# One attention band per query block instead of two: 128 wrapped weights, the 129th key in pass 3

## The chip, the cores and the metric

The kernel runs on one core of a Trainium2 chip. The metric is the device time of one launch in microseconds (us). TensorE (PE) multiplies matrices into PSUM banks, VectorE (DVE), ScalarE (ACT) and GpSimd (POOL) do the elementwise work, and SyncE (SP) issues every DMA of this kernel in one queue.

## The reference

One layer of a decoder for 2048 tokens of width 1024, in float32. After an RMS norm, one projection gives q, k, v and gate_B (8 heads of 64 each) and u, v, gate of a gMLP branch. The attention has three branches; each is a causal band over dilated keys:

```
DILATIONS = ((128, 1), (512, 4), (2048, 16))     # (window, dilation)
# query t attends t - dilation*j, j = 0..window/dilation  (129 keys: 128 back, and itself)
scores = q.k / 8;  keys outside the band or before the start are masked
out, lse = softmax per branch;  the three outs are summed with weights softmax(lse)
mixed = concat(attention * silu(gate_B), gmlp * silu(gate));  h = x + mixed @ w_out
h = h + sigmoid(RMSNorm(h) @ W_g + b_g) * (p @ W_p)
```

For a block of 128 queries the band covers parts of two key blocks: of its own block the keys up to the query, of the block behind it the keys from the query's position on. The 129th key (j = 128) lies at the query's own position in the block behind: 128 tokens back in branch 0, 512 in branch 1. In branch 2 the sequence has no block behind.

## The kernel before

Matrices are float32 numbers split into a high and a low part, so a projection of one 128-row tile to 512 columns is 24 matmuls of 128x512 (`project`, L230; `gm_product`, L633, in the gMLP).

- **Pass 1** takes 16 row tiles. `prep` norms and transposes a tile; `step` (four per tile, q k v g) projects it and hands the PSUM bank to `post_qk`, `post_v` or `post_gb`. The banks: q "mm" (2), k "s" (2), v and g take turns in "av" and "gt" (1 each). `turn_qk` transposes q and k by DMA (L434), copies k once more on ACT (L437) and stores both to DRAM.
- **The passage** into pass 2 loads and splits three gMLP weight groups (`load_group`, L136 and L138), and starts the gMLP products. The attention's buffers take the place of pass 1's.
- **Pass 2** has a hand-written order on PE (`manual_schedule`); the other engines follow the scheduler. There are 152 steps (4 head pairs x 3 branches). A step is one query block with both key blocks (108 of them), or one or two blocks with only their own key block; it has two heads and up to 512 weights per query row. `Step.scores`: 4 or 8 float16 matmuls (L762), a masked minimum from PSUM on DVE (L765), a constant added on DVE (L771), exp on ACT (L773). One step later `Step.turn`: a float16 copy on ACT (L780), the rest on POOL (L117), a DMA transpose to `pt` (L783). Six steps after the scores `Step.values`: 65-column matmuls (L794). After each `turn`, `fill(1.3)` puts gMLP matmuls of about 1.3 us into PE's order; `fill(18)` stands ahead of the first step. 13 of the 16 gMLP tiles run here, 3 after it (`tail`).
- **Pass 3** merges the three branches of a tile (`merge`: small DVE operations, L567, three POOL operations L569 to L572), transposes the result by DMA through the tiles `tm` (`turn_mixed`, L182 to L197) into the single buffer `aT`, and does `out_proj` and `gate`. The merge runs up to two tiles ahead.

Of the kernel before, what the change touches and what calls it, by code (L numbers as in the profile page):

```python
# [13 lines left out]
I32 = mybir.dt.int32  # L14
U16 = mybir.dt.uint16
# [21 lines left out]
def _shape_constants():  # L37

    p = np.arange(128)

    def mask(keys, back=False):
        keep = keys[None, :] >= p[:, None] if back else keys[None, :] <= p[:, None]
        return np.where(keep, 0, NEG).astype(np.float32)
    k0 = p.reshape(32, 4).T.reshape(128)
    return {"c_ident": np.eye(128, dtype=np.float32),
            "c_mask": np.concatenate([mask(k0, True), mask(k0), mask(p, True), mask(p)], 1),
            "c_freq": INV_FREQ.reshape(1, 32)}
# [3 lines left out]
PR, PH, OB, SV = 3, 6, 5, 5  # L51

LAG_B, LAG_C = 1, 6

BLOCK0, FILL = 18, 1.3
# [26 lines left out]
def hybrid_layer(ctx: ExitStack, tc: tile.TileContext, io, out):  # L82
# [17 lines left out]
    d_gb = dram.tile([S, 512], F32, name="d_gb")  # L100
    d_at = dram.tile([NT, 128, D], F32, name="d_at")
# [5 lines left out]
    cst.tile([128, 8], F32, name="pad")  # L107
    bs = cst.tile([128, 4], F32, name="bs")
# [13 lines left out]
    def load_group(src, c0, slot, stage, on_dve, each=None, gain=None):  # L122
# [3 lines left out]
        while k < nk:  # L126
# [5 lines left out]
            for i in range(n):  # L132
                hi, lo = slot[:, 0, k, :], slot[:, 1, k, :]
                if gain is not None:
                    nc.vector.tensor_scalar(raw[:, i], raw[:, i], gain[:, k:k + 1], None, op0=OP.mult)
                nc.scalar.activation(hi, raw[:, i], AF.Copy)  # L136
                dve = (k * on_dve) // 8 != ((k + 1) * on_dve) // 8
                (nc.vector if dve else nc.gpsimd).tensor_tensor(lo, raw[:, i], hi.bitcast(F32),  # L138
                                                                op=OP.subtract)
# [116 lines left out]

    AT, GT, XT, slots = {}, {}, {0: xt0}, {}
    usc = cst.tile([128, 1], F32, name="usc")

# [14 lines left out]
    with ExitStack() as s1, ExitStack() as s1q:  # L274
# [90 lines left out]
        def v_scale():  # L365
# [3 lines left out]
            ones = p1.tile([128, 128], F32, name="ones")  # L369
# [37 lines left out]
        def post_qk(n, which, ps):  # L407
# [8 lines left out]
            m1 = p1.tile([128, HEADS, 2, 32], F32, name="m1", bufs=2)  # L416
# [6 lines left out]
            pool_tt(f1, f1, f2, OP.add)  # L423
            r = m1.rearrange("p h t d -> p h (t d)")
            nc.vector.tensor_tensor(r, r, rs[:, :, None].to_broadcast([128, HEADS, 64]), op=OP.mult)
            hl = p1.tile([128, HEADS, 2, 64], F16, name="hl", bufs=2)
            nc.scalar.activation(hl[:, :, 0], r, AF.Copy)
            nc.vector.tensor_tensor(hl[:, :, 1], r, hl[:, :, 0], op=OP.subtract)
            return hl

        def turn_qk(n, which, hl):
# [3 lines left out]
            if which:  # L435
                sp = hl.rearrange("p h t d -> p h (t d)")
                nc.scalar.activation(sp.rearrange("p h (r i) -> p h r i", r=4),  # L437
                                     st.rearrange("p h (i r) -> p h r i", r=4), AF.Copy)
                st = sp
            nc.sync.dma_start(d_qk[which][:, n // 4, :, n % 4 * 128:n % 4 * 128 + 128], st)  # L440

        def post_v(n, ps):
# [4 lines left out]
            nc.scalar.activation(vt[:, :, 0, 0:64], z, AF.Copy, scale=sv)  # L447
            nc.vector.scalar_tensor_tensor(vt[:, :, 1, 0:64], z, sv, vt[:, :, 0, 0:64],
                                           op0=OP.mult, op1=OP.subtract)
            nc.sync.dma_start(d_vt[:, n * 128:(n + 1) * 128].rearrange("q p e -> p q e"),  # L450
# [3 lines left out]
        def post_gb(n, ps):  # L454
            g = p1g.tile([128, 512], F32, name="gb")
            nc.scalar.activation(g, ps, AF.Tanh, scale=0.5)
# [5 lines left out]
        def gm_constants():  # L462
            for name, src in (("mask", io["c_mask"]), ("wsT", d_ws),
                              ("lng", bcast(io["ln_v_g"], 512)), ("lnb", bcast(io["ln_v_b"], 512))):
                CG[name] = pg.tile([128, 512], F32, name=name)
                nc.sync.dma_start(CG[name], src)

        def spatial_weights():
# [4 lines left out]
            nc.sync.dma_start(keep[:, 0:128], io["c_mask"][:, 384:512])  # L473
# [486 lines left out]
```

## Time and profile before

| what | value |
|---|---|
| median of 3 runs | 1287.59 us (1286.81 to 1293.2) |
| profiled execution | 1287.08 us, span 1285.3 us, granted clock 0.985 |
| busy over the span | PE 93%, DVE 69%, ACT 50%, POOL 40% |
| DMA queue | 440432 packets, 232.44 MB |

Read it by stage. Pass 1 lasts to about 390 us, the passage to 430, pass 2 to 811, a second passage (the gMLP's last tiles, the weights of pass 3) to 950, pass 3 to the end. A share over the whole span mixes these.

### The profile page before, as it was taken

The numbers are of one execution on the slowest core, as the hardware profiler recorded it, in microseconds if no ns is written. First come the engines' busy times: TensorE is split into PE (matmuls) and PEld (weight loads), VectorE is DVE, ScalarE is ACT, GpSimd is POOL, SyncE is SP. The second block draws the span as 40 slices with busy tenths as digits, with TensorE's granted clock in tenths as the row PEclk, the third lists the DMA queues.
The fourth block names the chain that finished last, engine by engine and source line by source line (L and its number), as shares of the span: only waits on it lengthen the run. The fifth ranks groups of instructions, "written<-read, shape, count | busy, mean of one in ns | idle before, by whom it ended". The sixth has DMA issues, their size and how long they took to land.

```text
span 1285.3 us, 21313 instructions
## 1 busy us (share of the span) xinstructions
PE 1200.1 (93%) x7166; PEld 972.2 (76%) x7166; DVE 892.9 (69%) x2253; ACT 648.0 (50%) x1273; POOL 511.6 (40%) x454
## 2 busy tenths in 40 slices
PE   6899999999996899999899899869999999999998
PEld 4678787777785687777678688758778888888887
DVE  6895565565466588888778678598766776766733
ACT  5654433433335477777677677444334434434422
POOL 4762333343354365665555556342212212121200
PEclk9999999999999899999999999999999999999999
DMA  7498787768669989999999999845454565654531
GB/s 266 142 221 210 166 180 173 163 167 177 152 165 255 238 190 228 222 237 223 224 229 232 230 215 225 213 164 176 142 147 121 152 174 128 156 162 132 140 90 50
DMA packets 440542, 233.80 MB, mean 182 GB/s; under 512 B 337136, under 2 KB 389104, under 8 KB 440432
## 3 DMA queue, kind: packets, MB, share of 16 engines
q1 hardware_dynamic: 440432, 232.44, 75.5%
q8 instruction: 56, 0.92, 0.3%
q14 instruction: 54, 0.44, 0.1%
HBM read 102.99 MB, written 57.54 MB: 125 GB/s over the span
## 4 chain that ended last, share of the span: by engine, by line
PE 38%; DMA 21%; DVE 16%; ACT 8%; issue 7%; POOL 5%; SPq 4%; DVEq 0%; ACTq 0%; POOLq 0%
PE mm L230 17%; DMA pt<-raw 7%; PE mm L633 7%; PE gt L230 6%; DMA xt<-raw 3%; DMA st<-hl 3%; PE s L230 3%; PE s L762 2%; PE pt L794 2%; DVE wslot L138 2%; ACT pr L773 2%; ACT raw L182 2%; DVE raw L186 1%; DVE aT L197 1%; DMA raw<-w_in 1%
## 5 line engine op out<-in xcount | busy, mean ns | idle before, releaser
L230 PE MATMUL mm<-wslot,aT 128*128 128x512 f32 x1536 | 361.4, 390 | 5.1 <-ACT aT L196 1.9
L230 PEld LDWEIGHTS mm<-wslot,aT 128*128 128x128 f32 x1536 | 287.8, 188 | 67.8 <-ACT aT L196 3.4
L633 PE MATMUL mm<-wslot,aT 128*128 128x512 f32 x1152 | 312.7, 412 | 24.0 <-DVE gv L624 19.3
L633 PEld LDWEIGHTS mm<-wslot,aT 128*128 128x128 f32 x1152 | 210.3, 194 | 63.7 <-DVE gv L624 20.1
L117 POOL TENSOR_TENSOR raw<-pr,raw 128x512 f16<-128x512 f32 (+1 forms) x152 | 178.0, 1176 | 142.8 <-ACT raw L780 125.0
L230 PE MATMUL gt<-wslot,aT 128*128 128x512 f32 x744 | 183.9, 402 | 9.1 <-DVE gb L457 8.8
L773 ACT ACTIVATE pr<-pr,ost 128x256 f32<-128x256 f32 (+1 forms) x384 | 150.2, 451 | 72.2 <-DVE ost L771 66.6
L230 PEld LDWEIGHTS gt<-wslot,aT 128*128 128x128 f32 x744 | 143.5, 194 | 43.0 <-DVE gb L457 10.9
L794 PEld LDWEIGHTS <-pt 128*128 128x128 f16 x1800 | 64.9, 98 | 64.6 <-DMA pt<-raw 35.3
L780 ACT ACTIVATE raw<-pr 128x512 f16<-128x512 f32 (+1 forms) x152 | 93.1, 620 | 33.6 <-DMA pt<-raw 31.0
L794 PE MATMUL pt<-sv,pt 128*128 128x65 f16 x1800 | 82.0, 194 | 22.5 <-DMA pt<-raw 20.2
L765 DVE CUSTOM_DVE_ANT_0 pr<-s,mask 128x256 f32<-128x256 f32 (+1 forms) x256 | 81.1, 357 | 20.7 <-POOL raw L117 16.2
L230 PE MATMUL av<-wslot,aT 128*128 128x512 f32 x360 | 87.2, 394 | 7.5 <-DVE gb L457 4.1
L230 PE MATMUL s<-wslot,aT 128*128 128x512 f32 x384 | 91.0, 391 | 0.0
L117 POOL TENSOR_TENSOR m<-m,m 128x512 f32<-128x512 f32 x32 | 47.7, 1491 | 101.3 <-DVE rsh L150 95.0
L230 PEld LDWEIGHTS av<-wslot,aT 128*128 128x128 f32 x360 | 67.2, 188 | 24.9 <-DVE gb L457 6.0
L230 PEld LDWEIGHTS s<-wslot,aT 128*128 128x128 f32 x384 | 72.5, 189 | 15.3 <-ACT wslot L136 0.3
L572 POOL TENSOR_TENSOR ma<-ob,ma 128x512 f32<-128x512 f32 x16 | 23.8, 1488 | 123.4 <-DMA ma<-d_gb 87.3
L762 PEld LDWEIGHTS <-sq 128*128 128x128 f16 x768 | 70.1, 120 | 3.5 <-issue 1.6
L569 POOL TENSOR_TENSOR ob<-ob 128x512 f32<-128x512 f32 x16 | 21.0, 1314 | 128.8 <-DVE ob L567 128.8
L762 PE MATMUL s<-sk,sq 128*128 128x256 f16 (+1 forms) x512 | 72.3, 277 | 0.0
L771 DVE TENSOR_SCALAR ost<-ost 128x2 f32<-128x2 f32 (+1 forms) x152 | 65.4, 432 | 2.6
(198 smaller groups left out, 1730.0 us busy)
## 6 DMA issues: line engine op xcount, KB each, us to landing
xt<-x SPq DMA_DIRECT2D x32, 512.0 KB, 4.5
d_o<-ost SPq DMA_DIRECT2D x48, 264.0 KB, 3.7
raw<-w_in SPq DMA_DIRECT2D x38, 256.0 KB, 3.4
sv<-d_vt SPq DMA_DIRECT2D x32, 264.0 KB, 3.6
ob<-d_o SPq DMA_DIRECT2D x16, 528.0 KB, 4.6
xt<-d_at SPq DMA_DIRECT2D x16, 512.0 KB, 4.5
sk<-d_k SPq DMA_DIRECT2D x32, 256.0 KB, 4.8
out<-th SPq DMA_DIRECT2D x32, 256.0 KB, 2.8
```

The costliest lines, as they stand in the source:

```text
L117: nc.gpsimd.tensor_tensor(dst, a, b, op=op)
L138: (nc.vector if dve else nc.gpsimd).tensor_tensor(lo, raw[:, i], hi.bitcast(F32), op=OP.subtract)
L182: nc.scalar.activation(turned[t].bitcast(U16), words[:, t], AF.Copy)
L230: nc.tensor.matmul(ps, aT[:, ha, k, :], w(slot, hw, k), start=(n == 0), stop=(n == 3 * nk - 1))
L572: nc.gpsimd.tensor_tensor(m, o, m, op=OP.mult)
L633: nc.tensor.matmul(ps, GT[c][:, ha, k, :], slots[g][:, hw, k, :], start=(n == 0), stop=(n == 23))
L762: nc.tensor.matmul(ps[:, c:c + nk], cols(br, j, Q[h]), cols(br, j, K, n, h, self.nb), start=(n == 0), stop=(n == 1))
L765: nc.vector.tensor_tensor_reduce(pr[:, c:c + nk], ps[:, c:c + nk], mask[:, m - nk:m], -1.0, 3e38, op0=OP.add, op1=OP.min, accum_out=o[:, j ...
L771: nc.vector.tensor_scalar(nm, nm, math.log(PSCALE), None, op0=OP.add)
L773: nc.scalar.activation(pr[:, c:c + nk], pr[:, c:c + nk], AF.Exp, bias=o[:, j - j0, 130 + h:131 + h], scale=-1.0)
L780: nc.scalar.activation(ph, pr[:, :width], AF.Copy)
L794: nc.tensor.matmul(PO[0][:, j % 2, h], self.pt[:, t, c // 128], vt[:, h, vv, 0:65], start=(n == 0), stop=(n == 3 * self.nb - 1))
```

## The change

- **Wrapped band.** The scores of both key blocks are still computed. Where the own block's key lies after the query, DVE copies the score of the same column of the block behind over it in PSUM (`copy_predicated`), so 128 scores per query and head are left. DVE takes their maximum, ACT adds the constant, and ACT's exp reads PSUM.
- **Pairs.** Two row tiles share one `turn`: one float16 copy, one POOL subtraction, one DMA transpose for 512 weights. There are 192 steps and 96 turns.
- **Parting.** Five steps after the turn (`part`, for the 56 pairs with a block behind) DVE cuts the own block's weights out of `pt` into `pc` (a bitwise and over 32-bit words) and POOL subtracts them from `pt`. `values` multiplies `pc` with the own block's v and `pt` with the block behind's; the number of matmuls stays.
- **Far key.** Pass 1 multiplies q of a tile with k of the tiles 1 and 4 back (POOL), sums per head (DVE) and stores the 27 results; it also stores v in float32. Pass 3's merge takes the two scores as two more branches with denominator 1 and loads the rows of v: 1 or 2 more loads, 2 or 4 more POOL operations a tile, and some five more small DVE operations.
- **Pass 1.** g takes "pt" (2 banks) from the third tile on, so v has "av" and "gt" alone. The store of q and k (with ACT's copy of k) is issued behind the first ACT operation of the next step's `post`.
- **Passage.** The splits of the three gMLP weight groups come behind named operations of the last tiles' `post`. `fill` ahead of the first step is 11, after a step 0.93 (own block alone) or 1.17.

```diff
-LAG_B, LAG_C = 1, 6
-BLOCK0, FILL = 18, 1.3
+LAG_B, LAG_P, LAG_C = 1, 6, 9
+BLOCK0, FILL = 11, (0.93, 1.17)
...
+                with ExitStack() as behind:
+                    for ins in after:
+                        behind.enter_context(tc.issue_after(ins))
+                    nc.scalar.activation(hi, raw[:, i], AF.Copy)
...
+        def late(after):
+            for f in LATE:
+                with tc.issue_after(after):
+                    f()
+            LATE.clear()
...
+        def far_scores(n):
+            far = small.tile([128, 2, HEADS], F32, name="far", bufs=1)
...
+                    pool_tt(f, RT["k", n - back], RT["q"][1], OP.mult)
+                    nc.vector.tensor_reduce(far[:, x], t, axis=AX.X, op=OP.add, negate=True)
+            nc.sync.dma_start(d_far[n], far)
...
-            ps = bank({"q": "mm", "k": "s", "v": ("av", "gt")[n % 2], "g": "pt" if n >= NT - 2 else ("gt", "av")[n % 2]}[g])
+            ps = bank({"q": "mm", "k": "s", "v": ("av", "gt")[n % 2], "g": "pt" if n > 1 else ("gt", "av")[n]}[g])
...
+            nc.gpsimd.tensor_tensor(t, t, w[:, 3 + x][:, :, :, None].to_broadcast([128, 4, 2, 64]), op=OP.mult)
+            nc.gpsimd.tensor_tensor(o, o, t, op=OP.add)
...
+            def part(self, br, after):
...
+                with tc.issue_after(after.ins):
+                    nc.vector.tensor_tensor(d, a, bits[:, None, None, m:m + 64].to_broadcast([128, 2, 2 * n, 64]),
+                                            op=OP.bitwise_and)
+                pool_tt(a, a, d, OP.subtract)
...
+                    own = ps[:, :, 128:256]
+                    nc.vector.copy_predicated(own, m.bitcast(U32)[:, None].to_broadcast([128, 2, 128]),
+                                              ps[:, :, 0:128])
+                    self.last = nc.vector.tensor_reduce(top, own, axis=AX.X, op=OP.max, negate=True)
...
-                nc.vector.tensor_scalar(nm, nm, math.log(PSCALE), None, op0=OP.add)
+                nc.scalar.activation(top, top, AF.Copy, bias=math.log(PSCALE))
+                for h in range(2):
+                    nc.scalar.activation(pr[:, h], own[:, h], AF.Exp, bias=top[:, h:h + 1],
+                                         scale=1.0 if nb == 2 else -1.0)
...
+                if 0 <= n - LAG_P < len(plan) and steps[n - LAG_P].i:
+                    steps[n - LAG_P].pair.part(steps[n - LAG_P].br, steps[min(n, len(plan) - 1)].last)
```

## Rows read from the trace of the kernel before

**Rows 1.** Stages: stretch; us, busy us (instructions) per engine, clock, DMA share, GB/s.

```profile
90.00:390.00 300.00, 287.11 (x1241) 234.17 (x1240) 176.72 (x317) 120.74 (x201) 119.34 (x118) 0.99 0.75 176
390.00:430.00 40.00, 27.15 (x113) 22.01 (x113) 23.32 (x36) 18.83 (x31) 14.47 (x12) 0.83 0.89 241
430.00:811.00 381.00, 358.85 (x3484) 287.47 (x3483) 304.48 (x1191) 273.01 (x614) 228.91 (x199) 0.99 1.07 224
950.00:1250.00 300.00, 300.00 (x1325) 248.42 (x1324) 200.99 (x373) 120.16 (x219) 54.48 (x46) 1.00 0.54 144
```

**Rows 2.** Waits of PE, 90 to 390 us: total us, times, longest.

```profile
PE gt L230 <- DVE gb L457: 8.8, 5, 2.7
PE av L230 <- DVE gb L457: 4.1, 4, 1.4
```

**Rows 3.** Timeline of one pass 1 tile: start, us, instruction, idle before.

```profile
198.88 5.73 PE L230 MATMUL gt<-wslot,aT 128*128 128x512 f32 x24 [1.27 <-DVE gb L457]
...
222.25 2.11 PE L230 MATMUL av<-wslot,aT 128*128 128x512 f32 x8 [1.31 <-DVE gb L457]
```

**Rows 4.** Waits of ACT, 90 to 390 us.

```profile
ACT hl L437 <- DMA st<-hl: 38.3, 11, 4.9
```

**Rows 5.** Timeline of the passage.

```profile
395.96 11.04 PE L633 MATMUL mm<-wslot,aT 128*128 128x512 f32 x48
...
415.14 0.59 ACT L456 ACTIVATE gb<-pt 128x512 f32<-128x512 f32 x1
...
419.85 8.21 PE L633 MATMUL mm<-wslot,aT 128*128 128x512 f32 x24 [12.85 <-DVE gv L624]
...
423.06 0.80 SPq L264 DMA_DIRECT2D sq<-d_q  x2
```

**Rows 6.** Waits of PE's weight loads, 430 to 811 us.

```profile
PEld L794 <- DMA pt<-raw: 34.6, 33, 3.9
PEld L794 <- issue: 28.4, 104, 0.5
```

**Rows 7.** Timeline of PE's weight loads in one step of pass 2.

```profile
596.86 1.24 PEld L633 LDWEIGHTS mm<-wslot,aT 128*128 128x128 f32 x6
598.37 0.42 PEld L794 LDWEIGHTS <-pt 128*128 128x128 f16 x12 [0.27 <-issue]
```

**Rows 8.** Groups by form, 430 to 811 us: busy us, mean ns; idle before.

```profile
L117 POOL TENSOR_TENSOR raw<-pr,raw 128x512 f16<-128x512 f32 x146 | 173.1, 1190 | 130.1 <-ACT raw L780 112.4 <-POOL raw L117 5.6 <-issue 5.2
...
L780 ACT ACTIVATE raw<-pr 128x512 f16<-128x512 f32 x146 | 90.4, 626 | 33.5 <-DMA pt<-raw 31.0
...
L765 DVE CUSTOM_DVE_ANT_0 pr<-s,mask 128x256 f32<-128x256 f32 x144 | 55.2, 416 | 16.1 <-POOL raw L117 14.4 <-PE s L762 1.2
...
L771 DVE TENSOR_SCALAR ost<-ost 128x2 f32<-128x2 f32 x110 | 50.1, 457 | 1.8
...
L197 DVE TENSOR_TENSOR aT<-xt,aT 128x512 fp32r<-128x512 f32 x26 | 31.4, 1219 | 0.0
```

**Rows 9.** Groups by form, whole span.

```profile
L117 POOL TENSOR_TENSOR m<-m,m 128x512 f32<-128x512 f32 x32 | 47.7, 1491 | 101.3 <-DVE rsh L150 95.0 <-DVE m L420 6.2
...
L558 ACT ACTIVATE w<-w 128x24 f32<-128x24 f32 x16 | 3.6, 222 | 59.3 <-DVE w L557 59.3
```

**Rows 10.** DMA issues: count, median us to landing.

```profile
pt<-raw SPq DMA_TRANSPOSE x152, 4.1
```

**Rows 11.** Timeline of one pass 3 tile.

```profile
1021.39 0.77 ACT L196 ACTIVATE aT<-tm 128x256 fp32r<-128x256 f32 x2 [1.44 <-DVE tm L186]
...
1022.32 5.60 PE L230 MATMUL mm<-wslot,aT 128*128 128x512 f32 x24
...
1027.76 5.60 PE L230 MATMUL gt<-wslot,aT 128*128 128x512 f32 x24
...
1037.24 1.97 DVE L197 TENSOR_TENSOR aT<-tm,aT 128x256 fp32r<-128x256 f32 x2
...
1037.57 1.36 POOL L570 TENSOR_TENSOR ob<-ob 128x512 f32<-128x512 f32 x1
```

More of the change, by code (lines that the diff above doesn't have):

```diff
@@ L107, in hybrid_layer @@
     cst.tile([128, 8], F32, name="pad")
+    small.tile([128, 64], F32, name="pad", bufs=1)
     bs = cst.tile([128, 4], F32, name="bs")
@@ L589, in mixed @@
         nc.sync.dma_start(mx[0], d_gb[rows])
-        merge(ob, mx[0])
+        vr = pm.tile([128, D], F32, name="vr")
+        for x, back in enumerate(FAR):
+            if n >= back:
+                nc.sync.dma_start(vr[:, 512 * x:512 * x + 512], d_vr[(n - back) * 128:(n - back + 1) * 128])
+        merge(ob, mx[0], n, vr)
         AT[n] = mx
@@ L683, in gmlp @@
                     yield 0.43 if f is not gm_g else 1.28
[L685 to L686 removed]
+        for c, g, last in ((5, "va", (NT - 2, "k")), (4, "ua", (NT - 1, "k")), (6, "ga", (NT - 1, "v"))):
+            slots[g] = load_group(w_in, 512 * c, new_slot(), stage, WD2, after=POST[last])
         gm = gmlp()
@@ L754, in scores @@
             def scores(self):
                 Q, K = self.qk
-                br, nk, o, j0 = self.br, self.nk, self.o, self.j0
-                m = 512 if br else 256
-                ps = bank("s" if self.tick % 3 else "av")
-                self.pr = pr = p2.tile([128, 512], F32, name="pr", bufs=PR)
-                for c, j, h in self.segs:
-                    for n in range(2):
-                        nc.tensor.matmul(ps[:, c:c + nk], cols(br, j, Q[h]),
-                                         cols(br, j, K, n, h, self.nb), start=(n == 0), stop=(n == 1))
@@ new lines, in scores @@
+                m = mask[:, 128:256] if br else mask[:, 0:128]
+                ps = bank("s" if self.tick % 3 else "av")[:, 0:256 * nb].rearrange("p (h k) -> p h k", h=2)
+                pr = self.pair.pr[:, self.i]
+                for h in range(2):
+                    for n in range(2):
+                        nc.tensor.matmul(ps[:, h], cols(br, j, Q[h]),
+                                         cols(br, j, K, n, h, nb), start=(n == 0), stop=(n == 1))
+                top = o[:, j - j0, 130:132]
@@ new lines, in scores @@
+                if nb == 2:
+                    own = ps[:, :, 128:256]
+                    nc.vector.copy_predicated(own, m.bitcast(U32)[:, None].to_broadcast([128, 2, 128]),
+                                              ps[:, :, 0:128])
+                    self.last = nc.vector.tensor_reduce(top, own, axis=AX.X, op=OP.max, negate=True)
+                else:
+                    own = pr
+                    for h in range(2):
+                        self.last = nc.vector.tensor_tensor_reduce(
+                            pr[:, h], ps[:, h], m, -1.0, 3e38, op0=OP.add, op1=OP.min,
+                            accum_out=top[:, h:h + 1])
@@ L791, in values @@
+                if i == 0:
+                    PO[0] = bank("pt", (128, 2, 2, 65))
+                for h in range(2):
                     n = 0
-                    for vt in self.v[j]:
+                    for w, v in zip((self.pair.pc, self.pair.pt) if self.nb == 2 else (self.pair.pt,), self.v):
                         for t, vv in ((0, 0), (0, 1), (1, 0)):
-                            nc.tensor.matmul(PO[0][:, j % 2, h], self.pt[:, t, c // 128], vt[:, h, vv, 0:65],
+                            nc.tensor.matmul(PO[0][:, i, h], w[:, t, i, h], v[:, h, vv, 0:65],
@@ L805, in hybrid_layer @@
         quads = [(hp, br, j0) for hp in range(4) for br in (0, 2, 1) for j0 in range(0, NT, 4)]
-        plan = [(q, j) for q in quads for j in range(q[2], q[2] + 4, 2 if first(q[1], q[2] + 3) else 1)]
+        plan = [(q, j) for q in quads for j in range(q[2], q[2] + 4)]
         clock = [0.0, 0.0]
```

195 lines of the change are left out of this document (118 added, 77 removed).

## The prediction, made before the changed kernel was run

> **What bounds the kernel now.** I read the granted clock first (0.985, one core), then the stages, then in each stage what PE waits for. In pass 3 PE is busy all 300 of 300 us, and 24 matmuls follow the last 24 after 5.44 us (1022.32 to 1027.76), 227 ns each [rows 1, 11]. That is what a matmul of 128x512 costs when nothing is late, so nothing but later or fewer matmuls moves pass 3. In the other stages PE has holes: 12.9 us in pass 1, 12.9 us in the passage, where the clock is 0.83 besides, and 22.2 us in pass 2 [rows 1]. The change takes no matmul away. It can win only in those holes, 48 us and what the clock costs, and lose where it makes new ones.
>
> **Pass 1.** PE waits 12.9 us in nine places for DVE L457, g's last reader, to free the bank that v needs [rows 2]. From one v projection to the next it is 23.37 us (198.88 to 222.25), 4 x 5.44 = 21.76 are matmuls, so 1.6 us a tile is lost [rows 3]; over the eleven tiles 3 to 13 that is 18 us. Why is g's reader late? ACT stands 38.3 us in front of L437, until the DMA transpose of k has landed [rows 4], and g's tanh is queued behind it. The change treats both: g gets banks of its own, and L437 goes behind the next step's first ACT operation. Added in this pass are 27 products on POOL at about 1.49 us [rows 9], 40 us over 16 tiles beside 119 busy of 300 [rows 1]; 27 sums of 512 on DVE at no more than 1.22 us and 16 copies on ACT at 0.63 [rows 8]; two stores more per tile on SP, one of 256 KB and one of 8 KB. No engine gets near PE's 96%, so I count the work as hidden; without that cover the two products would put 3.0 us into the wait of k's rope on POOL. Bounds: 0 (something else in these in-order queues holds the 23.4 us) and -18. I take -13, nearer to the recorded idle.
>
> **The passage.** PE ends the first two gMLP products at 407 and waits 12.85 us for DVE L624, then runs 24 matmuls in 8.21 us in place of 5.6, at the lower of its two clock levels (1.2 GHz, the granted clock of the stretch is 0.83). The tanh of the last g tile, whose matmuls ended at 396, runs at 415.14, because ACT works through splits that wait for their loads; the attention's loads stand behind it on SP (423.06) [rows 5]. The change holds the splits back behind the last `post` operations and asks for 7 us less gMLP work ahead of the first step. If tanh comes 8 us sooner the loads do too, and PE, with less filler, still waits some of that. Bounds: -15 (wait and slow clock gone) and +7 (the loads come no sooner, and the 7 us of filler are missing). I take -6.
>
> **Pass 2, what goes.** PE's weight loads wait 34.6 us in 33 places for the transpose `pt` [rows 6]. Of each such wait 0.27 us would be there anyway (below), so 34.6 - 33 x 0.27 = 25.7 us are lost. The transposes compete in a DMA queue whose engines are busy 1.07 of the time, against 0.54 in pass 3 [rows 1]. 152 of them become 96 [rows 10], and with each of the 56 go an ACT copy (626 ns) and the POOL subtraction (1190 ns) that stand ahead of it [rows 8]. The lag from turn to use stays at about 14 us (7 steps of 2.0 us, before 5 of 2.4). So I count the 25.7 us as gained; if the DMA queue stayed full, none of it.
>
> **Pass 2, what comes on PE.** After a run of gMLP matmuls the next float16 weight load starts 0.27 us late, 104 times [rows 6]: six loads take 1.24 us, then 0.27 us pass, 1.51 for 6 x 0.227 = 1.36 us of matmuls [rows 7]. One more run thus costs 0.15 to 0.27 us, and 192 steps have 40 more than 152: 6 to 11 us, I take 8. The Trainium skill (TensorE: Matmul & The Clock Gate, Part 2) says that PE pulls the next weight load ahead of running matmuls; the rows show that it doesn't at this switch, and by the rule the sum would be 1254.
>
> **Pass 2, what comes beside it.** For a block with two key blocks DVE did two masked minima of 256 (416 ns each) and one constant (457) [rows 8]. Now it copies under a mask and reduces, both over 256 from PSUM. The trace has no masked copy: nearest is the minimum with a mask, 416 ns; it may cost the double if the target is read as well, and no row speaks for less. Half a `part` comes on top: 512 words with two SBUF inputs, 0.83 us at the minimum's rate and 1.22 by L197, which has two SBUF inputs as well [rows 8]. So 0.83 + 0.5 = 1.3 us against 1.29, in a step of about 2 us (381 / 192). The constant moves to ACT, 192 x 0.222 = 43 us [rows 9], against 152 x 0.45 = 68 on DVE. A two-element operation doesn't need 457 ns; it waits for something, and POOL is busy 60% of this pass [rows 1]. The Trainium skill (ScalarE: Activation LUTs, Rules for kernel authors) sends adds to VectorE; by these rows it is the dearer place here, and in neither case does it reach PE. POOL swaps 56 subtractions of 1.19 us for 56 over 32-bit words, between 1.2 and, for an unknown integer path, 3 us; I take the float row 1.49 [rows 9], +17 us on 229 of 381. The parting must be done in two steps after its scores; DVE (0.9 + 0.8 us) and POOL (1.5 us and a queue of about 1) need 4.2 of some 5.5 us (two steps and one more run of filler). That is thin. Queued behind a late `part` on DVE are the next scores' reductions, which free banks for PE. For new waits I take 8 us (56 parts at 0.15), bounds 0 and 40 (0.7 each). Sum of pass 2: -25.7 + 8 + 8 = -10, bounds -20 and +25.
>
> **Pass 3 and the passage before it.** The merge gets up to four POOL operations more (4 x 1.49 = 6 us a tile [rows 9]) and some five small DVE ones (1 us). POOL is busy 54 of 300 us [rows 1], so there is room, but not everywhere: `aT`'s first half was ready at 1022.16, out_proj started at 1022.32, 0.16 us of slack [rows 11]. DVE's L197, in front of the next transposes, took 1.97 us for two tiles of 256 while POOL ran L570 [rows 11]; more POOL work lengthens it. The merge's loads, two or three more per tile, stand on SP ahead of nothing that PE needs within a tile. Four is my estimate for both stages, bounds 0 and +36.
>
> **Sum**, against the profiled execution of 1287.1 us (the median of the runs shown is 0.5 above): 1287.1 - 13 - 6 - 10 + 4 = 1262.
>
> **Rivals.**
> - *Better throughout* (10%): all holes close. Pass 1 -18, passage -13, pass 2 -18, pass 3 0: 1238. For it: the waits named are few and the change touches each. Against: the thin margin of `part`.
> - *New waits take the place of the old in pass 2* (13%): the masked copy costs double or POOL's integer subtraction over 2.5 us, and the steps with two key blocks become bound by DVE or POOL. 108 of them at 0.14 us are +15 in place of -10: 1287, 1278 to 1292. For it: DVE 304 busy of 381 [rows 1]; against it: POOL's 112 us of waiting for ACT L780 [rows 8], room that the pairs leave.
> - *Slower, by the merge in pass 3* (12%): POOL's four operations fall just where DVE transposes the merged tile. If L197 and the copies behind it each wait for one more POOL operation, 3 us a tile, then twelve tiles lose 36 us with 0.16 to 2 us of slack: 1287 - 29 + 36 = 1294, up to 1305. It decides from 2.4 us a tile. For it: L197's 1.97 us; against: POOL's 54 us of 300 [rows 1], and three more of its operations a tile end before the next. The Trainium skill states the mechanism (GPSIMD Engine Reference, Key points): GpSimd shares its SBUF interfaces with VectorE where an instruction has two SBUF inputs. The trace agrees: 1.22 us for L197 at 512 elements in pass 2 [rows 8], 1.97 for two of 256 beside L570.
> - *Pass 1 doesn't get faster* (9%): the 23.4 us a tile are the loop through ACT, the DMA transposes and POOL, not the bank, and the products of the far key fill what `late` frees. 1262 + 13 = 1275, to 1285.
> - *No late start for the 40 new runs* (3 of the forecast's 56%): 8 us less, 1254. Against it stand 104 late starts [rows 6]; for it, that 48 of 152 runs show none of their own, most of them behind a wait for `pt`.
> - The forecast itself (56%): 1250 to 1276.
>
> **Numbers.** What a measurement here can tell from no change is about 0.5%, 6.4 us. Faster by more: the forecast 56, the better one 10, pass 1 held 5, new waits 3: 0.74. Within: 4 of pass 1, 8 of new waits, 2 of the merge: 0.14. Slower: 2 and 10: 0.12. The range of 1238 to 1293 leaves out some 5% below and 10% above; the forecast's own is 1250 to 1276.
>
> **What would show it.** Right: no wait of PE for L457, pass 1's projections of v 21.8 to 22.3 us apart; PE's first attention matmul before 415 us; 96 transposes, DMA share of pass 2 near 0.85, waits for `pt` under 10 us; some 40 more late starts of 0.27 us; PE without holes in pass 3. Wrong: waits of PE for `pt` or `pc` released by POOL's subtraction, a masked copy above 0.6 us, POOL integer work above 2 us, waits for `aT` in every tile of pass 3.

## The result, and the profile after

The changed kernel takes 1319.95 us (median of four runs, 1316.43 to 1324.45) against 1287.2 for the kernel before (four runs, 1285.2 to 1293.2): a ratio of 1.0252, 95% interval 1.0227 to 1.0277. It is slower by 2.5%; I had forecast 1262, faster by 2%. The profiled execution took 1316.43 us, its span 1314.7.

Read first by where the difference arises, with three marks that both traces have: PE's first attention matmul, the first product of the gMLP's tail, the end.

| stretch | before, us | after, us | difference |
|---|---|---|---|
| start to first attention matmul | 430.6 | 423.4 | -7.2 |
| pass 2 | 397.3 | 389.6 | -7.8 |
| tail of the gMLP, pass 3 | 457.4 | 501.8 | +44.4 |

Of the last row, 39.2 us arise in pass 3, behind a run of 48 matmuls that both have (at 934.4 and 924.6 us). The other 5.2 lie in the passage before it; no run looked into them. The stages of the changed kernel, as in [rows 1]:

```profile
90.00:390.00 300.00, 290.52 (x1271) 240.05 (x1270) 195.35 (x350) 127.22 (x212) 156.29 (x146) 0.98 0.78 191
390.00:430.00 40.00, 23.99 (x78) 16.20 (x77) 20.48 (x33) 21.51 (x40) 12.72 (x10) 0.74 1.01 276
430.00:811.00 381.00, 372.75 (x3596) 295.82 (x3595) 305.24 (x889) 259.94 (x751) 242.50 (x203) 1.00 0.86 190
950.00:1250.00 300.00, 273.50 (x1147) 221.52 (x1146) 203.40 (x375) 106.13 (x194) 118.07 (x87) 0.96 0.52 144
```

PE, busy 300 of 300 us in pass 3 before, is busy 273.5, at a clock of 0.96; POOL's busy time doubled from 54 to 118, no more than 40% of the stretch. What PE waits for there (all waits from 940 us on: total, times, longest):

```profile
PE mm L241 <- ACT aT L207: 23.2, 11, 5.2
PE mm L241 <- DVE xt L680: 3.5, 1, 3.5
```

Twelve times a projection waits for its operand or its bank. In five places the next 24 matmuls then take 7.35 to 8.59 us in place of 5.6, at a granted clock of 0.64 to 0.77 in these stretches, 10.9 us more together, so 26.7 us of waits cost 37.6. The longest of the five:

```profile
1109.14 8.59 PE L241 MATMUL mm<-wslot,aT 128*128 128x512 f32 x24 [4.36 <-ACT aT L207]
```

Pass 2 did what was asked of it. The waits of PE's weight loads, as in [rows 6], and the new forms, as in [rows 8]:

```profile
PEld L892 <- issue: 36.2, 133, 0.4
PEld L892 <- POOL pt L125: 6.1, 7, 2.2
PEld L892 <- DVE pc L837: 3.8, 3, 1.8
PEld L892 <- DVE ost L875: 2.2, 8, 0.3
PEld L892 <- DVE ost L871: 2.2, 8, 0.3
```

```profile
L125 POOL TENSOR_TENSOR pt<-pt,pc 128x512 int32<-128x512 int32 x52 | 67.9, 1307 | 50.1 <-issue 15.7 <-DVE pc L837 10.0 <-PE s L864 9.3
...
L837 DVE TENSOR_TENSOR pc<-pt,bits 128x512 int32<-128x512 int32 x52 | 48.3, 931 | 3.6 <-DMA pt<-raw 3.6
...
L879 ACT ACTIVATE ost<-ost 128x2 f32<-128x2 f32 x189 | 37.9, 200 | 90.3 <-DVE ost L871 59.2 <-DVE ost L875 29.5
...
L869 DVE COPY_PREDICATED s<-mask,s 128x256 f32<-128x256 uint32 x70 | 29.5, 421 | 4.8 <-PE s L864 4.0
```

No load waits for a transpose any more (33 did, 34.6 us); 29 more runs start late with nothing named (issue), 7.8 us in all; ten new waits, for POOL's subtraction and for `pc`, take 9.9 us. The rows that name another DVE operation, 34 loads and 9.3 us, have 0.27 us each: by their length the same late start. The masked copy costs 421 ns, the integer subtraction 1307.

Pass 1 has no wait for the bank [rows 2], and one new one, late:

```profile
PE mm L241 <- ACT aT L207: 9.5, 1, 9.5
```

### The profile page after: what moved, and what is told of

It is laid out like the page before. It is cut to its first block, busy times and chain, and to the rows that moved or that the text cites. A ratio compares the mean times of both kernels' runs of the same rounds, so it can differ in the third digit from the quotient of the medians.

```text
span 1314.7 us, 21431 instructions
## 1 busy us (share of the span) xinstructions
PE 1215.0 (92%) x7166; PEld 975.1 (74%) x7166; DVE 937.0 (71%) x2036; ACT 641.9 (49%) x1425; POOL 638.9 (49%) x535
## 5 line engine op out<-in xcount | busy, mean ns | idle before, releaser
L241 PE MATMUL mm<-wslot,aT 128*128 128x512 f32 x1536 | 378.2, 402 | 44.8 <-ACT aT L207 34.3
L705 PE MATMUL mm<-wslot,aT 128*128 128x512 f32 x1152 | 325.4, 417 | 16.6 <-ACT wslot L148 8.5
L125 POOL TENSOR_TENSOR raw<-pr,raw 128x512 f16<-128x512 f32 x96 | 115.7, 1205 | 71.9 <-ACT raw L821 44.3
L241 PE MATMUL gt<-wslot,aT 128*128 128x512 f32 x600 | 145.9, 397 | 0.2 <-ACT wslot L148 0.2
L637 POOL TENSOR_TENSOR vr<-vr,w 128x512 f32<-128x512 f32 x27 | 49.1, 1837 | 106.3 <-DVE w L626 106.3
L125 POOL TENSOR_TENSOR pt<-pt,pc 128x512 int32<-128x512 int32 (+1 forms) x56 | 70.9, 1266 | 55.4 <-issue 15.7
L879 ACT ACTIVATE ost<-ost 128x2 f32<-128x2 f32 x192 | 38.5, 200 | 93.2 <-DVE ost L871 60.5
L241 PE MATMUL pt<-wslot,aT 128*128 128x512 f32 x336 | 78.4, 389 | 0.0
L640 POOL TENSOR_TENSOR ma<-ob,ma 128x512 f32<-128x512 f32 x16 | 23.8, 1486 | 105.7 <-DMA ma<-d_gb 96.8
L241 PEld LDWEIGHTS pt<-wslot,aT 128*128 128x128 f32 x336 | 63.1, 188 | 13.1
L224 ACT ACTIVATE aT<-xt 128x1024 fp32r<-128x1024 f32 x32 | 34.0, 1061 | 66.3 <-DVE xt L680 63.9
L821 ACT ACTIVATE raw<-pr 128x512 f16<-128x512 f32 x96 | 60.4, 629 | 2.6
```

The costliest lines, as they stand in the source:

```text
L125: nc.gpsimd.tensor_tensor(dst, a, b, op=op)
L224: nc.scalar.activation(aT[:, 0].rearrange("p k t -> p (k t)"), xt, AF.Square, accum_out=ss)
L241: nc.tensor.matmul(ps, aT[:, ha, k, :], w(slot, hw, k), start=(n == 0), stop=(n == 3 * nk - 1))
L637: nc.gpsimd.tensor_tensor(t, t, w[:, 3 + x][:, :, :, None].to_broadcast([128, 4, 2, 64]), op=OP.mult)
L640: nc.gpsimd.tensor_tensor(m, o, m, op=OP.mult)
L705: nc.tensor.matmul(ps, GT[c][:, ha, k, :], slots[g][:, hw, k, :], start=(n == 0), stop=(n == 23))
```

## The experiments

Every ratio is to the kernel before, run on the same chip beside it; times are medians.

**Is it the merge, and which part of it?** The first run has the old merge (no far loads, no far weights); the second only loses these lines:

```diff
-            nc.gpsimd.tensor_tensor(t, t, w[:, 3 + x]..., op=OP.mult)
-            nc.gpsimd.tensor_tensor(o, o, t, op=OP.add)
```

> The changed kernel with the merge of the kernel before in pass 3: no loads of the far keys' scores and values there, weights for three blocks, none of the four added POOL operations. The far keys' share of the output is left out; pass 1 still computes and stores it. Pass 3 cost 390.1 us in the changed kernel against 350.9 before. Theory A (the merge is what costs) and theory B (its loads and small operations on DVE cost, not POOL's four operations) both expect pass 3 back at 350 to 356 us and 1276 to 1284 in all. Rival C (something that pass 1 or pass 2 leaves behind, such as the shorter slack of the output's loads, slows pass 3) expects 1305 or more.

> The changed kernel without POOL's two products and two sums of the far keys in pass 3; their loads, the weights for five blocks and all the small operations on DVE stay. The far keys' values are left out of the output. Theory A (POOL's four operations make DVE's copies and subtractions of the next tile late, and stand before POOL's own power for the norm) expects most of the 39 us back: 1278 to 1290. Theory B (loads on SP's queue and ten more small operations on DVE) expects 1308 to 1318.

Measured: 1277.66 us, ratio 0.990 (0.9871 to 0.993), and 1280.85, 0.9919 (0.9892 to 0.9947). Both lie in the ranges of theory A. Tail and pass 3 take 466.2 and 464.9 us against 501.8 (457.4 before). So four POOL operations a tile, 6.3 us of an engine that is idle 60% of the stretch, cost 37 us with all that waits behind them; the loads and small operations in pass 3 little or nothing. Groups of the run without them, 950 to 1250 us (busy us, mean ns), ahead of those of the changed kernel:

```profile
L208 DVE TENSOR_TENSOR aT<-tm,aT 128x256 fp32r<-128x256 f32 x48 | 29.0, 645 | 0.0
...
L629 DVE TENSOR_TENSOR ob<-ob,w 128x1536 f32<-128x1536 f32 x11 | 19.4, 1760 | 1.1
```

```profile
L637 POOL TENSOR_TENSOR vr<-vr,w 128x512 f32<-128x512 f32 x22 | 39.2, 1803 | 91.3 <-DVE w L626 91.3
L208 DVE TENSOR_TENSOR aT<-tm,aT 128x256 fp32r<-128x256 f32 x44 | 38.6, 918 | 0.0
...
L638 POOL TENSOR_TENSOR ob<-ob,vr 128x512 f32<-128x512 f32 x22 | 29.4, 1335 | 1.6
L629 DVE TENSOR_TENSOR ob<-ob,w 128x1536 f32<-128x1536 f32 x11 | 29.0, 2635 | 1.1
```

DVE's operations with two inputs in SBUF take 42 and 50% longer with POOL's four in the tile. The Trainium skill (GPSIMD Engine Reference, Key points) states that the two engines share SBUF interfaces and contend where a DVE instruction has two SBUF inputs, and here the trace agrees. But by the rows of one turn (below) it is some 1.7 us in a tile, and the tile is longer by more than that.

**Where in the tile?** One turn of the changed kernel, from L208 to L208 (the timeline; SPq are SP's issues; L208 is the L197 of [rows 11]). ob holds the tile's attention before the merge, vr the far values, ma the tile that the merged one is multiplied by and written to, tm its words for the transposes, xn the normed tile:

```profile
1013.64 2.77 DVE L208 TENSOR_TENSOR aT<-tm,aT 128x256 fp32r<-128x256 f32 x2
...
1016.21 2.72 POOL L638 TENSOR_TENSOR ob<-ob,vr 128x512 f32<-128x512 f32 x2
1016.50 1.15 ACT L193 ACTIVATE tm<-ma 128x512 uint16<-128x512 uint16 x2 [1.59 <-POOL ob L632]
1018.96 0.80 SPq L661 DMA_DIRECT2D vr<-d_vr  x2
1019.86 2.50 SPq L195 DMA_TRANSPOSE ma<-tm  x2
...
1022.47 2.60 SPq L195 DMA_TRANSPOSE xn<-turned  x2
1023.79 0.80 DVE L197 COPY tm<-ma 128x512 uint16<-128x512 uint16 x2 [2.97 <-DMA ma<-tm]
...
1025.08 0.75 DVE L208 TENSOR_TENSOR aT<-tm,aT 128x256 fp32r<-128x256 f32 x2
1025.23 0.47 SPq L657 DMA_DIRECT2D ma<-d_gb  x1
...
1028.21 1.65 POOL L640 TENSOR_TENSOR ma<-ob,ma 128x512 f32<-128x512 f32 x1 [8.77 <-DMA ma<-d_gb]
1029.88 0.38 SPq L652 DMA_DIRECT2D ob<-d_o  x1
...
1034.83 0.19 DVE L613 TENSOR_REDUCE mn<-ob 128x8 f32<-128x24 f32 x1 [1.43 <-DMA ob<-d_o]
...
1037.45 3.56 POOL L637 TENSOR_TENSOR vr<-vr,w 128x512 f32<-128x512 f32 x2 [7.59 <-DVE w L626]
1037.47 2.63 DVE L629 TENSOR_TENSOR ob<-ob,w 128x1536 f32<-128x1536 f32 x1
1040.03 0.68 DVE L680 TENSOR_TENSOR xt<-mm,xt 128x512 f32<-128x512 f32 x1
...
1041.23 2.75 DVE L208 TENSOR_TENSOR aT<-tm,aT 128x256 fp32r<-128x256 f32 x2
```

Most lines release the next, through single buffers (tm, ma, ob) and in-order queues. L638 with L661 is a branch that joins at the transposes; L637 and the short pair of L208 (1025.08, with POOL idle) are shown for L629 and the long pairs beside POOL. The profile puts ACT's L193 down to POOL's L632, which had ended 0.37 us before; in both kernels L193's operation starts 0.08 to 0.09 us after the end of L208, tm's last reader, and I take that for the releaser. It is 27.6 us from the end of one L208 to the next, where a tile's 108 matmuls need 24.48. The same turn in the kernel before took 23.06 (1062.22 to 1085.28), just short enough to hide:

```profile
1060.23 1.99 DVE L197 TENSOR_TENSOR aT<-tm,aT 128x256 fp32r<-128x256 f32 x2
...
1062.30 1.15 ACT L182 ACTIVATE tm<-ma 128x512 uint16<-128x512 uint16 x2 [0.80 <-POOL ob L570]
...
1063.47 2.50 SPq L184 DMA_TRANSPOSE ma<-tm  x2
...
1080.33 1.76 DVE L567 TENSOR_TENSOR ob<-ob,w 128x1536 f32<-128x1536 f32 x1
...
1083.42 1.86 DVE L197 TENSOR_TENSOR aT<-tm,aT 128x256 fp32r<-128x256 f32 x2
```

Of the 4.5 us more, L629 has 0.7 (it is 0.87 longer itself), L208 0.9, the small operations 0.7, and 2.2 are SP's: the words of the merged tile are ready at 1017.65, but ahead of their transposes stands the load of the far values, whose buffer POOL's last sum frees at 1018.93. I tried to take the pieces out one by one.

```diff
-        mx = [pm.tile([128, 512], F32, name=m) for m in ("ma", "mg")]
+        mx = [pm.tile([128, 512], F32, name=m, bufs=2 if m == "ma" else 1) for m in ("ma", "mg")]
```

> The changed kernel with two buffers in place of one for the tile that the merge multiplies by the gate (ma). The whole computation stands. In the changed kernel the merge's last operation on POOL waits about 9 us for that tile's load, which waits for the transposes of the tile before; only then is the attention's buffer free to be loaded, so the next merge falls on the moment at which DVE should subtract and copy for the next output projection. Theory A (the place of the POOL operations is what costs) expects the merge some 9 us earlier in its tile and 10 to 35 us back: 1281 to 1306. Rival B (the amount of work on POOL costs wherever it stands) expects less than 5 us: 1311 to 1318.

Measured: 1324.21, 1.0253 (1.0223 to 1.0282). Nothing won, above both ranges. The merges follow each other 27.05 us apart in the mean, and that mixes two rates: up to 1094 us L640 doesn't wait and they are 25.3 us apart, then 28.8, and L640 waits again for the gate's tile, whose load stands on SP behind the transposes (27.9 us in three places from 940 us on).

```diff
-        vr = pm.tile([128, D], F32, name="vr")
+        vr = pm.tile([128, D], F32, name="vr", bufs=2)
```

> The changed kernel with two buffers in place of one for the far keys' values in pass 3. The orders of PE, DVE, ACT and POOL stay as they are, and SP's nearly. In the changed kernel SP waits with the next tile's load of these values until POOL's last sum of the far keys has read the buffer (issue at 1018.96, that sum's end at 1018.93), and behind it stands the transpose of the merged tile, whose words ACT had ready at 1017.65 and which is issued at 1019.86: 2.2 us late, in the chain that out_proj waits for. Theory A (that wait on SP is most of the loss of pass 3): the transposes go out when ACT is done, 25 us or less a tile, waits for aT under 6 us, 20 to 38 us back: 1278 to 1297. Rival B (POOL's operations slow DVE's, which have two inputs in SBUF: L629 2.63 us against 1.76, L208 2.77 for two against 1.99, 1.65 us a tile): less than 12 us back: 1304 to 1316.

> The changed kernel with two buffers for the far keys' values and for the tile that the merge multiplies by the gate. With the second alone (two buffers for ma) the merge moved by several us and the time did not. If SP's wait for the far values' buffer is the loss, this one is within 6 us of the run with two buffers for the far values alone. If the orders that the planner then finds are worse by themselves, it stays near 1324.

Measured: 1318.32, 1.0205 (1.018 to 1.0231), just above rival B's range (to 1316); with both buffers doubled 1327.87 in a single run, near the run with ma alone. Theory A fell at once, by the trace of the first: with the second buffer SP merely loads a tile further ahead, at the same place in its queue, and waits for the same sum.

```profile
1073.52 2.71 POOL L638 TENSOR_TENSOR ob<-ob,vr 128x512 f32<-128x512 f32 x2
...
1076.26 0.80 SPq L661 DMA_DIRECT2D vr<-d_vr  x2
```

Then I queued the loads behind the transposes of the tile before, once with the order on POOL that the planner (the scheduler) then finds, once with POOL's products kept first:

```diff
+        with tc.issue_after(TURN[n - 1]) if n - 1 in TURN else ExitStack():
             for x, back in enumerate(FAR):
```

> The changed kernel with the loads of the far keys' values queued on SP behind the transposes of the merged tile before, in place of ahead of them. Two buffers alone did not help, because SP still issued the load of the next tile but one at that place and still waited for POOL's last sum (issue at 1076.26, that sum's end at 1076.23). The planner answers with another order on POOL: the two sums of the near blocks first, then the power for the norm, then the far keys' products and sums. The chain from the end of out_proj to the next one's first operand took 15.4 us in the run with two buffers, 10.5 before, and PE has 13.6 us of the gate's matmuls to cover it; of the 4.9 us more, 2.2 are SP's wait and 2.7 DVE (L629 later and longer, L208 longer). Theory A (either of the two alone stays within the 3.1 us of slack, both together don't): here both go, pass 3 at 350 to 358 us, no waits for aT above 1 us a tile, 1277 to 1288 in all. Rival B (POOL's 10 us a tile bind wherever they stand): waits of PE in most tiles, 1305 or more.

> As the run with the loads queued behind the transposes, but POOL's products of the far keys are kept ahead of its sums, so that they again run beside DVE's L629 and L208; SP's wait is gone. Theory A (slack of 3.1 us, DVE's part 2.7): few waits, 1280 to 1295. Rival (DVE's slowing is the loss, not SP's wait): as the changed kernel, 1308 to 1318.

Measured: 1329.24, 1.0312 (1.0279 to 1.0346), and 1353.66, 1.0485 (1.0442 to 1.0529). The first lies in rival B's range (1305 or more), the second above every range: now the merge waits for the late values ahead of its last product, ob comes free later, and merges follow each other 29.6 and 31.0 us apart. From the first of the two:

```profile
1081.48 1.13 POOL L639 TENSOR_TENSOR vr<-vr,w 128x512 f32<-128x512 f32 x1 [6.24 <-DMA vr<-d_vr]
...
1087.04 1.04 POOL L639 TENSOR_TENSOR vr<-vr,w 128x512 f32<-128x512 f32 x1 [2.75 <-DMA vr<-d_vr]
```

**Amount, place or queue?** Three runs, each with its own lines: half of the work; the loads on POOL's own queue; the work on DVE:

```diff
-            if n < back:
+            if x or n < back:                                  # one far key
-                nc.sync.dma_start(vr[:, ...], d_vr[...])
+                nc.gpsimd.dma_start(vr[:, ...], d_vr[...])     # POOL's queue
-            nc.gpsimd.tensor_tensor(t, t, ...); nc.gpsimd.tensor_tensor(o, o, t, ...)
+            nc.vector.tensor_tensor(t, t, ...); nc.vector.tensor_tensor(o, o, t, ...)   # on DVE
```

> The changed kernel with the second far key's product and sum taken off POOL in pass 3 (that key's value is left out of the output); all loads and weights stay, and PE's and ACT's orders too. Theory A (a closed loop of 27.6 us a tile against 24.5 us of matmuls): two operations less are 3.2 us less in the loop, 24.4 us, so nearly all of the loss comes back: 1279 to 1290. Rival B (POOL's amount of work counts in proportion): half of it, 1294 to 1302. Rival C (SP's wait for the buffer alone, whoever ends it): with the wait ended 3.2 us sooner it is gone as well, 1279 to 1290; the next run tells C from A.

> The changed kernel with the loads of the far keys' values issued from POOL's own queue in place of SP's, so that no transposes stand behind their wait for POOL's last sum. The whole computation stands. POOL does the same work plus these 27 issues. Rival C (SP's wait): the loss goes, 1278 to 1292. Theory A (the loop through the single buffers): SP's transposes no longer close it at that place, and the 2.2 us and the load's issue of 0.8 are out of it, so 24.6 to 25.5 us a tile, 1283 to 1300. Rival B (amount of POOL work, issues added): 1316 or more.

> The changed kernel with the far keys' products and sums in pass 3 done by DVE in place of POOL. The whole computation stands. By DVE's rows of 1.76 us for 1536 elements and 0.68 for 512 they take about 2.6 us a tile where POOL took 6.4, so the loop is 27.6 - 6.4 + 2.6 = 23.8 us, under the 24.5 of the matmuls; but they stand ahead of L208 in DVE's order, and the chain from out_proj to the next one's operand grows from 10.5 to some 13.1 of 13.6 us. Theory A: 1278 to 1290, at or below the kernel before. Rival B (DVE's order then makes the chain late): 1295 to 1310.

Measured: 1292.52, 1.002 (1.0004 to 1.0037); 1318.77, 1.0227 (1.02 to 1.0255); 1303.92, 1.0111 (1.0083 to 1.0138). The second and third lie in the ranges of their rivals B. The mean distance of L640 from tile to tile orders these runs (first and last of eleven between 960 and 1260 us):

| kernel | us a tile | ratio |
|---|---|---|
| before | 23.85 | 1 |
| no POOL operations | 24.20 | 0.9919 |
| one far key | 26.13 | 1.002 |
| both keys on DVE, ahead of L208 | 27.37 | 1.0111 |
| loads on POOL's queue | 27.95 | 1.0227 |
| changed kernel | 28.04 | 1.0252 |

Each key puts 1.9 us into the loop for 3.1 us of POOL work (28.04, 26.13, 24.20): in proportion, as rival B has it, above what the matmuls cover; the time, 1292.5, lies between A's range (to 1290) and B's (from 1294). The run with POOL's own queue shows why SP's wait alone was worth nothing:

```profile
1074.32 2.50 SPq L195 DMA_TRANSPOSE ma<-tm  x2
...
1078.93 2.58 SPq L195 DMA_TRANSPOSE xn<-turned  x2
1081.68 0.46 SPq L657 DMA_DIRECT2D ma<-d_gb  x1
```

The transposes now go out as soon as ACT is done, 2.2 us sooner in the loop. But the power for the norm (L162) stands on POOL behind the four operations, so xn comes 3.0 us after its sum (before: 0.66), its transposes go out late, and behind them the load of the gate's tile. So a second path of nearly the same length lay beside the first. Both were taken out at once, and DVE's version was moved behind L208:

```diff
-        nc.sync.dma_start(mx[0], d_gb[rows])
+        nc.gpsimd.dma_start(mx[0], d_gb[rows])                 # beside vr's loads there
+        with tc.issue_after(LAST[n - 1, 1]):                   # the other run: DVE, behind L208
+            nc.vector.tensor_tensor(t, t, ...); nc.vector.tensor_tensor(o, o, t, ...)
```

> The changed kernel with the loads of the far values and of the gate's tile issued from POOL's queue; the orders of the other engines stay. With the far values' loads alone there nothing was gained: SP's wait of 2.2 us went, but the gate tile's load then stood behind the transposes of xn, which POOL's late power holds back by as much. Here both are out of SP's queue. Theory A (the loop): 1 to 2 us a tile less, for L629 and L208 beside POOL, and SP's own transposes ahead of the attention's load, stay in it: 25.5 to 26.6 us a tile, 1298 to 1312. Rival B (SP's waits are all of it): 1280 to 1292. Rival C (SP's queue has no part): 1314 or more.

> The changed kernel with the far keys' products and sums in pass 3 done by DVE, as in the run that gave 1.011, but issued behind L208 of the tile before (the subtraction that the next output projection's transposes wait for) in place of ahead of it; the planner then also puts the loads of the far values behind the transposes. The whole computation stands. The loop that I read from the trace (L208, ACT's copy of the merged tile, SP's transposes, the load of the gate's tile, the merge's last product, the attention's load, the merge's small operations, L629, L680, L208) takes 23.0 us a tile in the kernel before, 27.6 in the changed one, and 24.5 us are matmuls. Theory A (that loop binds): without POOL's four operations only the 0.7 us of added small operations stay in it, 23.7 us; DVE's 3 us stand in a stretch where it waited for POOL's power and the transposes. Pass 3 352 to 358 us, 1280 to 1288 in all, a ratio of 0.992 to 0.998 to the kernel before. Rival B (the amount of work on DVE counts wherever it stands): as the run with it ahead of L208, 1.007 to 1.014.

Measured: 1316.1, 1.0183 (1.0153 to 1.0213), in rival C's range (1314 or more). The merges are 27.11 us apart, 0.9 of the 3.8 us a tile less, but tail and pass 3 together are only 1.4 us shorter (500.4 against 501.8); the issues now take 2.0 us of POOL's time a tile, so the run doesn't price SP's wait alone. And 1293.59, 1.0013 (0.9998 to 1.0029): the same work at another place in DVE's queue (and the far values' loads behind the transposes) is 1% cheaper, as fast as the kernel before within 0.3%, and 0.9% above the run without the work; neither theory's range holds it. What comes late there is the norm again, behind DVE's sums:

```profile
1063.11 1.28 DVE L638 TENSOR_TENSOR vr<-vr,w 128x512 f32<-128x512 f32 x2
1064.32 0.14 DVE L161 TENSOR_SCALAR rs<-ss 128x1 f32<-128x1 f32 x1
1064.38 0.68 DVE L639 TENSOR_TENSOR ob<-ob,vr 128x512 f32<-128x512 f32 x1
1065.50 0.75 DVE L229 TENSOR_SCALAR xn<-xt,rs 128x1024 f32<-128x1024 f32 x1 [0.44 <-POOL rs L162]
```

The distance does not order every run: 27.05 us stand at 1.0253 (two buffers for ma), 27.11 at 1.0183 (both loads on POOL's queue), 26.60 at 1.0013 (DVE behind L208). PE's own waits from 940 us on follow the times more closely: 1.7 us without POOL's operations, 12.9 with DVE behind L208, 13.1 with one far key, 19.4 with DVE ahead, 23.6 with both loads on POOL's queue, 26.7 in the changed kernel, 30.4 with the far loads there alone, 37.3 with two buffers for ma.

**Pass 1.** One line of the change in the kernel before, all orders kept:

```diff
-"g": "pt" if n >= NT - 2 else ("gt", "av")[n % 2]
+"g": "pt" if n > 1 else ("gt", "av")[n]
```

> The kernel before with one line of the change: from the third tile on g's projection goes into the bank pt, so that v never waits for g's reader. All orders are those of the kernel before. My prediction took the bank's wait as the loss of pass 1 (12.9 us of waits, 13 taken). If so, 1272 to 1278, 1.0% faster. Rival (a loop of 23.2 us a tile through ACT, DVE, POOL and the DMA transposes is what holds pass 1; the changed kernel has no wait for the bank and still turns its tiles 23.2 us apart): PE runs ahead for some tiles and then waits for a late tile, pass 1 ends less than 7 us sooner, 1281 to 1288.

Measured: 1284.82, 0.9964 (0.9939 to 0.9988), in the rival's range, 0.4% faster than the kernel before. The nine waits for L457 [rows 2] are gone, and in their place stands, as in the changed kernel:

```profile
PE mm L230 <- ACT aT L196: 10.5, 1, 10.5
```

PE ran ahead at 21.76 us a tile while tiles were turned 23.7 us apart, until the last was late. Three runs of the changed kernel looked for what holds the turns: no far products in pass 1; v's constant columns written by POOL only four times; and that with the products behind k's rope sum.

```diff
-            vt = p1.tile([128, HEADS, 2, 66], F16, name="vt", bufs=2)
-            nc.gpsimd.memset(...)
+            vt = VT[n if n < 4 else 2 + n % 2]     # memset for n < 4 alone
-                if RT["q"][0] == n + which <= RT["k"][0] + 1:
-                    far_scores(n + which)
+                if which:
+                    with tc.issue_after(POST[n, "k"][2]):
+                        far_scores(n)
```

> The changed kernel without the far keys' products (POOL, 27 times) and sums (DVE, 27 times) in pass 1; the far scores are stored as the constant that gives weight 0, and v is stored as in the changed kernel. The far keys so drop out of the output. PE runs without a hole to 339 us and then waits 9.5 us for the last tile's transposes, because the loop through ACT, DVE, POOL and the DMA transposes takes 23.2 us a tile where PE needs 21.76. Theory A (POOL's 3.45 us of products a tile lengthen that loop) expects the loop at 22.5 us or less, the hole under 3 us, pass 1 ended 8 to 12 us sooner. How much of it is left at the end depends on the passage: if the attention's loads follow pass 1, 1304 to 1310; if the splits of the next weights hold them, 1313 to 1318. Rival B (the new stores on SP and the held back operations make the loop, not the products) expects the hole unchanged within 2 us and 1314 to 1318.

> The changed kernel with the constant columns of v's tile (a 0 and a 1 beside each head) written by POOL for the first four tiles alone, which then keep two buffers in turn. The orders of all engines stay, but for POOL's 24 short memsets. In the changed kernel POOL's memset waits for the store of the tile before the last from that buffer (d_vp, issued by SP behind the late store of q and the far scores' store), and behind it in POOL's queue stands the power for the norm of the next tile (L162 at 337.77, memset 337.70), so that a tile's turn takes 23.2 us where PE needs 21.76. Theory A (this wait closes the loop): the turns come 22 us apart or less, the 9.5 us hole before the last q projection is under 3 us, pass 1 ends 7 to 12 us sooner. The total follows by 3 to 12 us: 1304 to 1313. Rival B (the loop runs through the queue of ACT and the DMA transposes, and POOL's wait is only beside it): the hole changes by less than 2 us, 1314 to 1318.

> The changed kernel with v's constant columns written for the first four tiles alone, and the far keys' products of pass 1 issued on POOL behind the rope sum of the same tile's k in place of ahead of it. With the first edit alone the turns still came 22.6 to 23.9 us apart; the loop then ran through POOL's two products (3.47 us), which stand ahead of k's power and rope sum, and by these through DVE's k operations to the norm of the next tile. Theory A (the products in that place close the loop): turns 22 us apart or less, hole before the last q projection under 3 us, first attention matmul at 412 to 418 in place of 423.4, total 3 to 10 us less: 1306 to 1313. Rival B (the planner's order of the other engines makes a loop of about 23 us whatever is taken out): hole within 3 us of 9.5, 1313 to 1320.

Measured: 1331.43, 1.0312 (1.0286 to 1.0337); 1317.5, 1.0187 (1.0156 to 1.0217); 1352.32, 1.0491 (1.046 to 1.0521). Turns 24.4, 22.9 and 25.3 us apart (changed kernel 23.3); the second, the only one with all other orders kept, cut the hole from 9.5 to 8.3 us, as its rival B had it; the other two miss all their ranges. With fewer or later products the planner ordered ACT's and DVE's queues anew, and PE's holes grew to 18.7 and 18.1 us, so these two don't say what the products cost. That pass 1 is held by turns of some 23 us and not by the bank is shown; which link of that loop to cut is open.

The two combinations brought nothing of their own:

> Both of the two edits: two buffers for the far keys' values in pass 3, and the constant columns of v's tile written for the first four tiles alone. The whole computation stands. If each removes its own wait, the gains add: 1270 to 1285, faster than the kernel before. If the first gives 20 us or less, 1290 to 1300. If pass 1's gain is swallowed by the loads of the passage, it is like the first alone within 3 us.

> Both: pass 1 as in the run with the products behind k, pass 3 as in the run with the loads behind the transposes. The whole computation stands. If both theories A hold, 1268 to 1280, faster than the kernel before by 0.8 to 1.6%. If only pass 3's holds, 1277 to 1288.

Measured: 1318.48, 1.0202 (1.0179 to 1.0226), and 1362.56, 1.0571 (1.054 to 1.0602), slower than either of its parts.

## Why the prediction was wrong

- **Pass 3, the step that failed.** "Four is my estimate for both stages" measured +44, 39 of it in pass 3. The bound of +36 and the rival that named the merge had the mechanism half right: DVE's L629 and L208 slow down beside POOL. I had read 0.16 us of slack and given that rival 12%, since POOL was idle 82% of the time and "three more of its operations a tile end before the next". An idle engine was the wrong thing to look at: a turn that passes through it took 23.06 of 24.48 us, 1.4 us of slack for 6.3 us of new work.
- **SP in pass 3.** "The merge's loads ... stand on SP ahead of nothing that PE needs within a tile" was false; the load waits for POOL's last sum with the transposes behind it. By the rows of one turn this is 2.2 of the 3.8 us a tile that POOL's operations cost, and DVE's slowing 1.6. The runs don't confirm that division: with both loads on POOL's queue the merges came 0.9 us a tile closer and the stretch only 1.4 us shorter. That POOL's four operations cost the 37 us is shown; how these divide between SP's queue, the norm behind POOL and DVE's slowing stays open.
- **Pass 1.** -13 taken, about -6.5 measured: the waits went as forecast, v's projections came 21.76 us apart, and 9.5 us came back in one place, with 24 matmuls in 8.3 us in place of 5.6 behind them. The loop through ACT, transposes and POOL that my rival "pass 1 doesn't get faster" named ate half of the gain, where the rival had it eat all. The one line for the bank alone ends pass 1 6.1 us sooner, so the late stores and far products together changed next to nothing.
- **The passage.** -6 taken, -0.7 measured (34.6 to 33.9 us). The first attention matmul still waits, 7.55 us for a load of v, with the DMA engines busy 1.01 of the stretch (before 0.89). My sum also forgot that gMLP matmuls taken from the passage must run elsewhere: 80 became 52 ahead of the first score, and pass 2 has 956 in place of 929. So the passage lost its 28 matmuls and hardly got shorter. No run tried the passage alone.
- **Pass 2.** -10 taken, -7.8 measured with 27 matmuls (6.1 us) more in it. Like for like that is 13.9 us against 10 taken. Each term held within its bounds: all waits for `pt` gone; late starts, counted with those put down to DVE and those inside waits, 137 before and 177 now, the 40 more that I had reckoned with, 10.8 us of the loads' time at 0.27 us each (8 taken); new waits 9.9 us less the 0.27 us that ten starts have anyway, 7.2 (8 taken); masked copy 0.421 us, integer subtraction 1.31 (1.49 taken), DMA share 0.86. But with the 25.7 us of the old waits these add up to 7.7 us and not to 13.9, so a late load costs PE less than its 0.27 us, or a term is missing; no run shows which. The Trainium skill (TensorE: Matmul & The Clock Gate, Part 2) states that PE pulls the next weight load ahead of running matmuls where the row groups don't conflict or the load goes to the background buffer; at this switch the rows show no such gain, and the 104 late starts without a named cause became 133.

## What to carry to other kernels

Slack is a property of a loop, not of an engine: before adding work to an idle engine, follow one buffer around (last reader, queue of the reload, what stands behind it) and compare the loop's time with the tile's matmuls. A busy PE hides loops that are almost as long; and where two queues carry the same delay, taking out one shows nothing, so test them together, and see that the test puts no work of its own into the loop. When PE's wait goes away in a pipelined stage, look whether the producer was slower anyway: PE then runs ahead and pays in one place.

## What the runs showed that I had not expected

A second buffer did not free SP's queue: the load was issued at the same place and waited for the same reader, one tile further ahead (1076.26 against POOL's end at 1076.23). The same 2.6 us of DVE work cost 1.0% more ahead of a subtraction than behind it (1.0111 against 1.0013), though SP's order differed as well. And 27 us of PE's waits cost 38, because the runs of 24 matmuls behind them took up to 8.59 us in place of 5.6.
